# A hybrid diffusion block on one Trainium2 core: the low part of most weight tiles comes from an accumulating DMA instead of a VectorE subtraction

## The chip, the core and the metric

The kernel runs on one core of a Trainium2 chip. The metric is the time of one execution on the device, in microseconds (us). The engines are named as the profile names them: PE is TensorE (PEld its weight loads), DVE is VectorE, ACT is ScalarE, POOL is GpSimd, SP is SyncE, which here only issues DMAs. L12 is line 12 of the kernel's file; before and after have their own line numbers.

## What is computed

One layer of a diffusion backbone over 512 latent tokens of width 1024, with 256 context tokens in front of a state-space scan. All weights are float32, and the result is compared with a float32 reference. Cut to what matters:

```python
z, xbc, dt_raw, cv_in, pool_in, gate_logits = split(h @ w_in)         # latent and context
y_ssd  = rms_norm(ssd_scan(silu(conv5(xbc)), dt) * silu(z)) @ ssd_w_out
y_conv = silu(layer_norm(depthwise_conv31(a * sigmoid(b)))) @ cv_w_out  # a, b = cv_in
y_pool = pool_mixer(pool_in)
g = sigmoid(gate_logits)
x = x + mod[2] * ((g0 * y_ssd + g1 * y_conv + g2 * y_pool) @ w_out)
x = x + mod[5] * ((silu(h2 @ w_gate) * (h2 @ w_up)) @ w_down)
return rms_norm(x, final_g)
```

The change touches how the tiles of `w_in`, `cv_w_out`, `ssd_w_out`, `w_out` and `w_down` are made ready for the matmuls.

## The kernel before

Activations lie with channels on the 128 partitions and tokens along the free dimension, 512 wide. Every product is made of two-part numbers: a float32 value is split into a rounded float32r part `hi` and the rest `lo`, and a product is `hi*hi + hi*lo + lo*hi`, three matmuls (`mm3`, L136 to L138). A weight tile has 128 output channels and 1024 inputs (768 for `wcv` and for each third piece of `wdn`), so a whole tile takes 8 times 3, that is 24, matmuls of 128x512.

`load_unit` (L117) makes such a tile: an SP DMA brings 512 KB from HBM into `raw` (tag "wr"), ACT rounds it to `hi` (tag "whi"), DVE subtracts, `lo = raw - hi` (tag "wlo"). Each tag has three buffers, so the parts of a tile can be written only when the matmuls of the tile three before it are done. In the program's text the stages are:

- start (to about 48 us): the modulation, the first norm, three tiles of `win` split by hand (`first_split`), which the change leaves alone;
- 50 to 325 us: tiles of `win` for convolution, pooling and `xbc` (L755), with DVE at work on the 31-tap convolution (`conv31`, L410), pooling and the 5-tap convolution (L702);
- 325 to 500 us: tiles of `win` for `z` and the gates (`spill_tile`), spilled to HBM, between them the scan (`ssd_gen`): per chunk a product `cb` on PE (L820), `cbd` on DVE (L826), `xd` on POOL (L830);
- 500 to 625 us: `wcv`, `wso` and `wout` tiles; beside them the spilled gates and branch sums come back (L975, L976), rows of `wada` are read for the second modulation (`ada`, L902), and `x`, `yd` are read;
- 625 to 835 us: the gate and up projections, which the change leaves alone (`ffn_unit`, `fast_pair`);
- 835 us to the end: the down projection, 24 pieces of `wdn`, then the last norm and the output.

The order of the work on each engine comes from a scheduler with priorities (`later` pushes work back; `tc.high_priority()` puts the rounding and subtraction of a tile early). Each engine then runs its own instructions in that order. POOL has 68 instructions: pads set to zero (L398, L462, L657, L760) and the eight `xd` products.

Of the kernel before, what the change touches and what calls it, by code (L numbers as in the profile page):

```python
# [10 lines left out]
AF = mybir.ActivationFunctionType  # L11
ALU = mybir.AluOpType  # L12
P = 128
# [14 lines left out]
I_CV, I_PL, I_XBC, I_Z, I_G1, I_G0 = 0, 12, 26, 38, 46, 54  # L28
# [25 lines left out]
def hybrid_block(ctx, tc, x, cx, cck, cc, wad, wada, vec, prm, cst, inv, onehot, win, wdt, wcv, wpl, wso, wout, wgu, wdn, out):  # L54
    nc = tc.nc
# [9 lines left out]
    V, S, PE = (Ordered(e) for e in (nc.vector, nc.scalar, nc.tensor))  # L65
# [7 lines left out]
    def nm(s):  # L73
        uid[0] += 1
        return f"{s}_{uid[0]}"

    def pt(pool, shape, tag, bufs, dt=F32):
        return pool.tile(shape, dt, tag=tag, name=nm(tag), bufs=bufs)

    def mmp():  # L80
        return pt(psum, [P, T], "mm", 3)
# [4 lines left out]
    def tmp():  # L86
        return pt(per, [P, T], "tmp", 4)
# [24 lines left out]
    def load_raw(src, n):  # L112
        raw = pt(per, [P, 1024], "wr", 3)
        nc.sync.dma_start(raw[:, :n], src)
        return raw

    def load_unit(src, n=1024, urgent=True):  # L117
        raw = load_raw(src, n)
        hi = pt(per, [P, 1024], "whi", 3, F32R)
        lo = pt(per, [P, 1024], "wlo", 3, F32R)  # L120
        with tc.high_priority():
            S.copy(hi[:, :n], raw[:, :n])  # L122
            if urgent:
                V.tensor_tensor(lo[:, :n], raw[:, :n], hi[:, :n], ALU.subtract)  # L124
        if not urgent:
            V.tensor_tensor(lo[:, :n], raw[:, :n], hi[:, :n], ALU.subtract)
        return hi, lo

    def split(dst_hi, dst_lo, src):
        S.copy(dst_hi, src)  # L130
        V.tensor_tensor(dst_lo, src, dst_hi, ALU.subtract)  # L131

    def mm3(o, w, col, rhs, first, last):
        hi, lo = w
        rh, rl = rhs
        PE.matmul(o, hi[:, col : col + P], rh, start=first, stop=False)  # L136
        PE.matmul(o, hi[:, col : col + P], rl, start=False, stop=False)  # L137
        PE.matmul(o, lo[:, col : col + P], rh, start=False, stop=last)  # L138
# [20 lines left out]
    def slot_a(dt=F32):  # L159
        return pt(f1, [P, 2, T], "A", 3, dt)  # L160
# [10 lines left out]
    def slot_c(dt=F32):  # L171
        return pt(f1, [P, 1024], "C5", 4, dt)
# [167 lines left out]
    V, S, PE = nc.vector, nc.scalar, nc.tensor  # L340
# [10 lines left out]
    def drain(gen):  # L351
        for _ in gen:
            pass

    @contextmanager
    def later(n):
        keep = tc.cur_priority
        tc.cur_priority = keep + n
        yield
        tc.cur_priority = keep  # L360

    def win_tile(i, bank=mmp):
        if pre:
            return pre.pop(0)
        w = load_unit(win[i])
        o = bank()
        for k in range(KT):
            mm3(o, w, k * P, hh[k], k == 0, k == KT - 1)
        return o
# [47 lines left out]
    def conv_steps(n, ins=None):  # L417
        with ExitStack() as st:
            st.enter_context(later(100000))
            if ins is not None:  # L420
                st.enter_context(tc.issue_after(ins.ins))
            while n and convs:
                if next(convs[0], 0) == 0:
                    convs.popleft()
                else:
                    n -= 1
# [325 lines left out]

    tails = []
    for q, i in enumerate((8, 9, 10, 11, 0, 1, 2, 3, 4, 5, 6, 7)):
        w = load_unit(win[I_XBC + q])  # L755
        o = mmp()
        for k in range(KT):
            mm3(o, w, k * P, hh[k], k == 0, k == KT - 1)
        pad = slot_c()
        nc.gpsimd.memset(pad[:, 0:2], 0.0)  # L760
        nc.gpsimd.memset(pad[:, 514:518], 0.0)
        S.copy(pad[:, 2:514], o)
        if i < 10:
            oc = mmp()
            for k in range(KT):
                mm3(oc[:, :TC], w, k * P, hc[k], k == 0, k == KT - 1)
            nc.gpsimd.memset(pad[:, 774:776], 0.0)
            S.copy(pad[:, 518:774], oc[:, :TC])
        conv_steps(CONV_STEPS_XBC[q], mark[-1])
        while len(tails) > TAILS_KEPT_XBC[q]:  # L770
            drain(tails.pop(0))
        tails.append(xbc_tail(i, pad))
        next(tails[-1], None)
# [121 lines left out]
    def ada(n=1):  # L895
        for _ in range(n):
            if not adas:
                return
            chunk, t = adas.popleft()
            raw = load_raw(wada[(chunk - 2) * 8 + t], 1024)  # L900
            i = chunk * 8 + t
            V.tensor_tensor_reduce(  # L902
                raw, raw, silb[0], 1.0, vc("b_ada", i), ALU.mult, ALU.add, mod_l[:, i : i + 1]
            )
# [22 lines left out]
    with later(100000):  # L927
        cvy = []
        for j in range(6):
# [3 lines left out]
            hi, lo = p[:, 0:T], p[:, T : 2 * T]  # L933
            split(hi, lo, f)
            cvy.append((hi, lo))
    with later(9000):
        for m in range(8):
            w = load_unit(wcv[m], 768)
            oc = mmp()
            for k in range(6):  # L940
                mm3(oc, w, k * P, cvy[k], k == 0, k == 5)
            sp = tmp()
            S.copy(sp, oc)
            nc.sync.dma_start(mrg[:, m, 1, :], sp)
            ada(1)
# [6 lines left out]
    for t in range(KT):  # L952
# [5 lines left out]
        hi, lo = pt(per, [P, T], "hh", 8, F32R), pt(per, [P, T], "hl", 8, F32R)  # L958
# [8 lines left out]
        mg.append((slot_w(F32R), slot_w(F32R)))  # L967

    for m in range(8):
        w = load_unit(wso[m])  # L970
        o = mmp()
        for k in range(KT):
            mm3(o, w, k * P, y_hl[k], k == 0, k == KT - 1)
        ga, mo = slot_a(), slot_c().rearrange("p (a b) -> p a b", b=T)
        nc.sync.dma_start(ga, gat[:, m])  # L975
        nc.sync.dma_start(mo, mrg[:, m])  # L976
        S.activation(ga, ga, AF.Sigmoid)
        V.tensor_tensor(mo[:, 1, :], mo[:, 1, :], ga[:, 1, :], ALU.mult)
        V.tensor_tensor(mo[:, 0, :], mo[:, 0, :], mo[:, 1, :], ALU.add)
        V.tensor_tensor(ga[:, 0, :], o, ga[:, 0, :], ALU.mult)  # L980
        V.tensor_tensor(mo[:, 0, :], mo[:, 0, :], ga[:, 0, :], ALU.add)
        mr = mo[:, 0, :]
        split(mg[m][0], mg[m][1], mr)
# [6 lines left out]
    def project(o, ws, rhs, sl):  # L990
        n = sum(kn for _, kn in ws)
        q = 0
        for w, kn in ws:
            for k in range(kn):
                mm3(o[:, sl], w, k * P, tuple(a[:, sl] for a in rhs[q]), q == 0, q == n - 1)
                q += 1

    def residual(m, o, gate, base, sl, q, ms=None):
        V.scalar_tensor_tensor(x1[:, m, sl], o[:, sl], gate, base[:, sl], ALU.mult, ALU.add)
        if ms is None:  # L1000
            sq_acc(acc[:, sl], x1[:, m, sl], m == 0, sl.stop - sl.start, q)
        else:
            S.activation(q[:, sl], x1[:, m, sl], AF.Square)
            PE.matmul(ms, mean, q[:, sl], start=False, stop=True)

    def rms_head(sl):
        ms = psp()[:, : sl.stop - sl.start]
        PE.matmul(ms, mean, acc[:, sl], start=True, stop=False)
        return ms

    def rms_tail(ms, sl):
        rnorm(ms, sl.stop - sl.start, acc[:, sl])

    def wout_tile(m):
        if m % 2 == 0:
            xp.append(slot_a())
            nc.sync.dma_start(xp[-1], x[:, m : m + 2, :])
        return load_unit(wout[m]), mmp()

    xp, up = [], []  # L1020
    nh = 8 - WOUT_HALVED
# [16 lines left out]
    for m in range(nh):  # L1038
        if m < 2:
            o = pair[m][1]  # L1040
        else:
            w, o = wout_tile(m)
# [185 lines left out]
    for q in range(NFF // 2):  # L1228
# [3 lines left out]
        for e in range(2):  # L1232
            if tags:
                hi, lo = (a[:, e, :] for a in pair)
            else:
                hi, lo = (pt(per, [P, T], "hh", 8, F32R) for _ in range(2))
# [5 lines left out]
    for m in range(8):  # L1242
        ada(1)
        o = mmp()
        ws = [(load_unit(wdn[m, :, k0 * P : (k0 + kn) * P], kn * P), kn) for k0, kn in ((0, 8), (8, 8), (16, 6))]
        for sl in halves if m == 7 else whole:
            ms = rms_head(sl) if m == 7 else None
            project(o, ws, hid, sl)
            residual(m, o, mod_l[:, 40 + m : 41 + m], x1[:, m, :], sl, pt(per, [P, T], "hl", 8), ms)
            S.activation(x1[:, m, sl], x1[:, m, sl], AF.Copy, scale=fin_n[:, m : m + 1])  # L1250
            if m < 7:
                continue
            rms_tail(ms, sl)
            n = T // 2
            for q in range(4):
                ot = pt(f2, [P, 2, n], "hid", NFF)
                V.tensor_tensor(
                    ot, x1[:, 2 * q : 2 * q + 2, sl], acc[:, sl].unsqueeze(1).to_broadcast([P, 2, n]), ALU.mult
                )
                nc.sync.dma_start(out[:, 2 * q : 2 * q + 2, sl], ot)  # L1260
# [124 lines left out]
```

## Time and profile before

| | before |
|---|---|
| median of 3 runs | 984.8 us (983.79 to 985.79) |
| the profiled execution | 984.63 us |
| its span in the trace | 982.9 us |
| PE busy | 961.0 us (98%) |
| DVE busy | 781.8 us (80%) |
| ACT busy | 465.6 us (47%) |
| POOL busy | 20.7 us (2%) |
| DMA queue of SP | 143.23 MB, 43.8% of 16 engines' span |

The span runs from the first to the last instruction of the trace; 1.7 us of the execution lie around it. A busy PE in this table is not a PE at its peak: a 128x512 matmul is shown as 0.39 us long, but the next one starts 0.23 us later. "Share" of DMA is the mean busy share of the core's 16 DMA engines.

### The profile page before, as it was taken

Reading aid. Unit: us, or ns where it says so; the run is one execution under the profiler, and the core shown is the slowest. Engines: PE = TensorE matmul, PEld = TensorE weight load, DVE = VectorE, ACT = ScalarE, POOL = GpSimd, SP = SyncE. Lnnn points to the kernel's source line nnn. Section 1 sums busy time; section 2 is a strip of 40 time slices with the busy share of each in tenths; the row PEclk is TensorE's granted clock in tenths of the full one; section 3 lists DMA queues with packets and bytes.
Section 4 is the critical chain, followed back from the end, with each engine's and each line's share of the span. In section 5 each row is a group of like instructions: output and inputs, shape, how many; then the busy total and the mean of one; then the engine's idle time right before and its main releaser. Section 6 shows DMA issues by size and latency. Waiting matters only on the chain.

```text
span 982.9 us, 14243 instructions
## 1 busy us (share of the span) xinstructions
PE 961.0 (98%) x5468; PEld 807.9 (82%) x5468; DVE 781.8 (80%) x1196; ACT 465.6 (47%) x710; POOL 20.7 (2%) x68
## 2 busy tenths in 40 slices
PE   6999999999999999999999999999999999999996
PEld 4678888888887777766688788989999999888885
DVE  5589999977889999999987864999888888743333
ACT  5683643335445243245664544655555556432331
POOL 0100000000000000100100000000000000000000
PEclk9999999999999999999999999999999999999998
DMA  9653335322123356654769963233233333443422
GB/s 363 268 184 103 115 115 161 107 86 65 65 59 102 108 177 221 201 165 141 217 227 305 340 207 126 86 108 120 96 109 107 108 108 107 128 148 107 139 81 86
DMA packets 59157, 144.15 MB, mean 147 GB/s; under 512 B 11728, under 2 KB 22608, under 8 KB 57936
## 3 DMA queue, kind: packets, MB, share of 16 engines
q1 hardware_dynamic: 59088, 143.23, 43.8%
q8 instruction: 43, 0.70, 0.3%
q14 instruction: 26, 0.21, 0.1%
HBM read 126.44 MB, written 16.78 MB: 146 GB/s over the span
## 4 chain that ended last, share of the span: by engine, by line
PE 88%; DVE 5%; DMA 3%; ACT 1%; issue 1%; SPq 0%; DVEq 0%; ACTq 0%
PE mm L137 19%; PE mm L136 19%; PE mm L138 19%; PE mm L1162 10%; PE ps L1162 8%; PE mm L63 1%; DMA wr<-in_wso_dram 1%; PE ps L1079 1%; PE ps L796 1%; DMA wr<-in_wada_dram 1%; PE y L866 1%; PE ps L855 1%; PE ps L63 1%; PE ps L748 1%; DVE A L410 1%
## 5 line engine op out<-in xcount | busy, mean ns | idle before, releaser
L138 PE MATMUL mm<-hh,wlo 128*128 128x512 f32 (+1 forms) x612 | 242.5, 396 | 0.5 <-DVE wlo L124 0.5
L136 PE MATMUL mm<-hh,whi 128*128 128x512 f32 (+1 forms) x612 | 242.3, 396 | 0.3 <-ACT whi L122 0.3
L137 PE MATMUL mm<-hl,whi 128*128 128x512 f32 x576 | 230.2, 400 | 0.0
L122 ACT CAST whi<-wr 128x1024 fp32r<-128x1024 f32 (+1 forms) x115 | 117.0, 1021 | 237.6 <-PE mm L137 184.4
L124 DVE TENSOR_TENSOR wlo<-wr,whi 128x1024 fp32r<-128x1024 f32 (+1 forms) x112 | 132.0, 1181 | 54.5 <-ACT whi L122 54.0
L138 PEld LDWEIGHTS mm<-hh,wlo 128*128 128x128 f32 x612 | 115.2, 188 | 28.8 <-issue 4.3
L136 PEld LDWEIGHTS mm<-hh,whi 128*128 128x128 f32 x612 | 115.2, 188 | 27.3 <-issue 3.0
L137 PEld LDWEIGHTS mm<-hl,whi 128*128 128x128 f32 x576 | 108.4, 188 | 26.0 <-issue 4.3
L410 DVE SCALAR_TENSOR_TENSOR A<-U,vec_t,A 128x512 f32<-128x512 f32 x180 | 128.0, 752 | 0.0
L1162 PE MATMUL mm<-T,shi 128*128 128x256 f32 x288 | 53.5, 283 | 0.0
L130 ACT CAST shi<-S 128x1024 fp32r<-128x1024 f32 x36 | 37.8, 1050 | 31.8 <-DVE S L1150 26.1
L702 DVE SCALAR_TENSOR_TENSOR C<-C,vec_t,C 128x772 f32<-128x772 f32 (+1 forms) x48 | 46.9, 977 | 4.8 <-ACT C L700 2.2
L131 DVE TENSOR_TENSOR slo<-S,shi 128x1024 fp32r<-128x1024 f32 x36 | 44.1, 1225 | 5.9 <-ACT shi L130 5.9
L1162 PEld LDWEIGHTS mm<-T,shi 128*128 128x128 f32 x288 | 44.9, 191 | 0.0
L130 ACT CAST whi<-wr 128x1024 fp32r<-128x1024 f32 (+1 forms) x36 | 30.1, 836 | 25.9 <-PE ps L1162 21.2
L1162 PE MATMUL mm<-T,slo 128*128 128x256 f32 x144 | 40.9, 284 | 0.0
L131 DVE TENSOR_TENSOR wlo<-wr,whi 128x1024 fp32r<-128x1024 f32 (+1 forms) x36 | 34.5, 958 | 7.1 <-ACT whi L130 5.5
L136 PE MATMUL mm<-H,whi 128*128 128x256 f32 (+1 forms) x124 | 37.4, 302 | 0.0
L137 PE MATMUL mm<-H,whi 128*128 128x256 f32 (+1 forms) x124 | 37.3, 300 | 0.0
L138 PE MATMUL mm<-H,wlo 128*128 128x256 f32 (+1 forms) x124 | 37.2, 300 | 0.0
L902 DVE CUSTOM_DVE_ANT_0 wr<-wr,C,vec_t 128x1024 f32<-128x1024 f32 x24 | 30.7, 1279 | 1.0 <-DMA wr<-in_wada_dram 0.9
L902 DVE CUSTOM_DVE_ANT_0 wr<-wr,sil_f,vec_t 128x1024 f32<-128x1024 f32 x8 | 10.3, 1283 | 23.6 <-DMA wr<-in_wada_dram 23.6
(396 smaller groups left out, 2070.7 us busy)
## 6 DMA issues: line engine op xcount, KB each, us to landing
wr<-in_win_dram SPq DMA_DIRECT2D x62, 512.0 KB
wr<-in_wgu_dram SPq DMA_DIRECT2D x44, 512.0 KB
wr<-in_wada_dram SPq DMA_DIRECT2D x32, 512.0 KB
wr<-in_wdn_dram SPq DMA_DIRECT2D x16, 512.0 KB
X<-in_wad_dram SPq DMA_DIRECT2D x4, 1024.0 KB
H<-in_wad_dram SPq DMA_DIRECT2D x4, 1024.0 KB
mrg<-tmp SPq DMA_DIRECT2D x16, 256.0 KB
gat<-tmp SPq DMA_DIRECT2D x16, 256.0 KB
```

The lines of the kernel that those rows point to most:

```text
L63: return lambda *a, **k: tc.keep_in_program_order(op(*a, **k))
L122: S.copy(hi[:, :n], raw[:, :n])
L124: V.tensor_tensor(lo[:, :n], raw[:, :n], hi[:, :n], ALU.subtract)
L130: S.copy(dst_hi, src)
L131: V.tensor_tensor(dst_lo, src, dst_hi, ALU.subtract)
L136: PE.matmul(o, hi[:, col : col + P], rh, start=first, stop=False)
L137: PE.matmul(o, hi[:, col : col + P], rl, start=False, stop=False)
L138: PE.matmul(o, lo[:, col : col + P], rh, start=False, stop=last)
L410: V.scalar_tensor_tensor(accs[e], pads[e](k), vc("dw_w", (2 * j + e) * 31 + k), accs[e], ALU.mult, ALU.add)
L702: tap = V.scalar_tensor_tensor(a[:, 0:n], pad[:, k : n + k], vc("conv_w", i * 5 + k), a[:, 0:n], ALU.mult, ALU.add)
L902: V.tensor_tensor_reduce(raw, raw, silb[0], 1.0, vc("b_ada", i), ALU.mult, ALU.add, mod_l[:, i : i + 1])
L1162: PE.matmul(o[:, left], x[:, cs], rhs[k][y], start=first and k + n == 0, stop=k == 3 and n == 2, skip_group_check=True,)
```

## The change

`load_unit` gets a flag `rmw`, set at six of its callers: the tiles of `win` that are not split by hand (59), of `wcv` (8), `wso` (8), `wout` (8) and the pieces of `wdn` (24), 107 in all. With the flag ACT writes `hi` as before and then a second pass, `lo = -raw`, rounded in the same way by the float32r output; then a DMA issued by POOL reads the same weight tile from HBM once more and adds it to `lo`. The five tiles of the plain gate and up projections that are not first (`urgent`) keep the DVE subtraction.

```diff
-    def load_unit(src, n=1024, urgent=True):
+    def load_unit(src, n=1024, urgent=True, rmw=False):
         raw = load_raw(src, n)
         hi = pt(per, [P, 1024], "whi", 3, F32R)
         lo = pt(per, [P, 1024], "wlo", 3, F32R)
+        if rmw:
+            with tc.high_priority():
+                S.copy(hi[:, :n], raw[:, :n])
+                S.activation(lo[:, :n], raw[:, :n], AF.Copy, scale=-1.0)
+            nc.gpsimd.dma_start(lo[:, :n], src, accum_op=ALU.add)
+            return hi, lo
...
-        w = load_unit(win[i])
+        w = load_unit(win[i], rmw=True)
...
-        w = load_unit(win[I_XBC + q])
+        w = load_unit(win[I_XBC + q], rmw=True)
...
-            w = load_unit(wcv[m], 768)
+            w = load_unit(wcv[m], 768, rmw=True)
...
-        w = load_unit(wso[m])
+        w = load_unit(wso[m], rmw=True)
...
-        return load_unit(wout[m]), mmp()
+        return load_unit(wout[m], rmw=True), mmp()
...
-        ws = [(load_unit(wdn[m, :, k0 * P : (k0 + kn) * P], kn * P), kn) for k0, kn in ((0, 8), (8, 8), (16, 6))]
+        ws = [(load_unit(wdn[m, :, k0 * P : (k0 + kn) * P], kn * P, rmw=True), kn) for k0, kn in ((0, 8), (8, 8), (16, 6))]
```

The scheduler places the new instructions, and it shifts others around them. ACT at the `wso` tiles, before: `wr_...` are the raw tiles, `A_...` the gates, `C_...` the merged rows that become `H_...`.

```order
L977 ACTIVATE A_4743<-A_4743 128x1024
L130 CAST H_4618<-C_829_4660 128x512
L122 CAST whi_4756<-wr_4754 128x1024
L977 ACTIVATE A_4785<-A_4785 128x1024
L130 CAST H_4618<-C_835_4702 128x512
L122 CAST whi_4798<-wr_4796 128x1024
```

The same place after:

```order
L983 ACTIVATE A_4813<-A_4813 128x1024
L136 CAST H_4685<-C_829_4728 128x512
L123 CAST whi_4869<-wr_4867 128x1024
L124 ACTIVATE wlo_4870<-wr_4867 128x1024
L136 CAST H_4685<-C_835_4771 128x512
L983 ACTIVATE A_4856<-A_4856 128x1024
L983 ACTIVATE A_4899<-A_4899 128x1024
```

Behind each rounding of a tile now stands the second pass, which writes `wlo`; the other ACT work keeps its place but for one gate pass.

POOL between the pads of the scan's set-up (`M_...`, L657 before and L663 after) and those of the pooling (`X_...`), before:

```order
L657 MEMSET M_900 128x512
L657 MEMSET M_904 128x512
L657 MEMSET M_932 128x512
L657 MEMSET M_936 128x512
L462 MEMSET X_459 128x256
L463 MEMSET X_459 128x256
```

And after, from the last two accumulating DMAs ahead of the fourth pad:

```order
L125 DMA wlo_1108<-in_win_dram 128x1024
L125 DMA wlo_1152<-in_win_dram 128x1024
L663 MEMSET M_941 128x512
L125 DMA wlo_1198<-in_win_dram 128x1024
L125 DMA wlo_1253<-in_win_dram 128x1024
L468 MEMSET X_459 128x256
L125 DMA wlo_1287<-in_win_dram 128x1024
L469 MEMSET X_459 128x256
```

Accumulating DMAs that PE waits for now stand in one row with pads that wait for PE and DVE.

PE at the first tile that `load_unit` makes (`mm_472` before, `mm_473` after; `ps_567`, `ps_568` is the small product for `dt`), before:

```order
L63 MATMUL mm_209<-hh_95,wlo_345 128x512
L273 MATMUL ps_567<-W_106,C_61_269 32x512
L136 MATMUL mm_472<-hh_81,whi_468 128x512
L137 MATMUL mm_472<-hl_82,whi_468 128x512
L138 MATMUL mm_472<-hh_81,wlo_469 128x512
```

And after:

```order
L279 MATMUL ps_568<-W_116,C_61_269 32x512
L279 MATMUL ps_568<-W_118,C_61_269 32x512
L279 MATMUL ps_568<-W_120,C_61_269 32x512
L142 MATMUL mm_473<-hh_81,whi_468 128x512
L143 MATMUL mm_473<-hl_82,whi_468 128x512
L144 MATMUL mm_473<-hh_81,wlo_469 128x512
```

All eight products for `dt` now stand ahead of the tile; of each tile the third matmul is the first that reads `wlo`.

## Rows read from the trace of the kernel before

**Rows 1.** Page, busy time of each engine: us, share of span, instructions.

```profile
PE 961.0 (98%) x5468; PEld 807.9 (82%) x5468; DVE 781.8 (80%) x1196; ACT 465.6 (47%) x710; POOL 20.7 (2%) x68
```

**Rows 2.** Waits of PE: total us, times, longest.

```profile
PE ps L63 <- DMA X<-in_wad_dram: 8.2, 2, 7.2
PE mm L1162 <- DVE wlo L131: 1.3, 1, 1.3
...
PE ps L796 <- DVE W L794: 0.5, 2, 0.4
PE mm L138 <- DVE wlo L124: 0.5, 1, 0.5
```

**Rows 3.** Busy time by stage: from:to, length, engines, PEclk, DMA share, GB/s.

```profile
50.00:325.00 275.00, 274.61 (x1409) 228.24 (x1408) 248.49 (x370) 130.02 (x199) 5.42 (x46) 1.00 0.34 104
325.00:500.00 175.00, 174.46 (x801) 123.95 (x800) 165.25 (x271) 77.13 (x117) 11.91 (x8) 1.00 0.55 177
500.00:575.00 75.00, 74.21 (x326) 60.44 (x325) 60.29 (x88) 40.44 (x53) 0.00 (x0) 1.00 0.90 313
575.00:625.00 50.00, 49.91 (x293) 44.23 (x292) 26.96 (x47) 25.06 (x43) 0.00 (x0) 1.00 0.31 105
835.00:960.00 125.00, 124.95 (x579) 104.03 (x578) 56.99 (x74) 41.40 (x54) 0.00 (x0) 1.00 0.38 120
```

**Rows 4.** Costliest groups: the subtraction, the rounding, the scaled pass.

```profile
L122 ACT CAST whi<-wr 128x1024 fp32r<-128x1024 f32 (+1 forms) x115 | 117.0, 1021 | 237.6 <-PE mm L137 184.4
L124 DVE TENSOR_TENSOR wlo<-wr,whi 128x1024 fp32r<-128x1024 f32 (+1 forms) x112 | 132.0, 1181 | 54.5 <-ACT whi L122 54.0
L977 ACT ACTIVATE A<-A 128x1024 f32<-128x1024 f32 x8 | 8.5, 1061 | 10.0 <-DMA A<-gat 9.8
```

**Rows 5.** The subtractions (L124) of each stage.

```profile
50.00:325.00 275.00, 46.84 (x39) 1.00 0.34 104
325.00:500.00 175.00, 25.94 (x22) 1.00 0.55 177
500.00:575.00 75.00, 17.09 (x16) 1.00 0.90 313
835.00:960.00 125.00, 28.37 (x25) 1.00 0.38 120
```

**Rows 6.** SP's DMA queue, 500 to 575 us: packets, MB, share.

```profile
q1 hardware_dynamic: 7785, 23.38, 89.9%
```

**Rows 7.** Chain of waits, 500 to 545 us: start, us, what.

```profile
517.20 5.29 DMA wr<-in_wada_dram
522.51 1.28 DVE wr L902
...
524.54 8.18 DMA wr<-in_wso_dram
...
535.21 6.09 DMA wr<-in_wso_dram
541.38 1.06 ACT whi L122
542.46 1.24 DVE wlo L124
```

**Rows 8.** A load in the down projection: its issue on SP, its reader.

```profile
873.10 0.33 SPq L114 DMA_DIRECT2D wr<-in_wada_dram  x1
...
876.61 1.28 DVE L902 CUSTOM_DVE_ANT_0 wr<-wr,sil_f,vec_t 128x1024 f32<-128x1024 f32 x1 [3.55 <-DMA wr<-in_wada_dram]
```

**Rows 9.** ACT in order of time: roundings that wait for a free buffer.

```profile
45.52 1.05 ACT L122 CAST whi<-wr 128x1024 fp32r<-128x1024 f32 x1 [0.58 <-PE mm L63]
...
93.00 1.05 ACT L122 CAST whi<-wr 128x1024 fp32r<-128x1024 f32 x1 [2.57 <-issue]
98.49 1.05 ACT L122 CAST whi<-wr 128x1024 fp32r<-128x1024 f32 x1 [4.45 <-PE mm L137]
...
103.94 1.04 ACT L122 CAST whi<-wr 128x1024 fp32r<-128x1024 f32 x1 [3.90 <-PE mm L137]
...
861.18 1.05 ACT L122 CAST whi<-wr 128x1024 fp32r<-128x1024 f32 x1 [4.39 <-PE mm L137]
865.26 0.84 ACT L122 CAST whi<-wr 128x768 fp32r<-128x768 f32 x1 [3.03 <-PE mm L137]
```

**Rows 10.** PE and POOL in order of time, around the waits of POOL.

```profile
48.39 1.05 PE L273 MATMUL ps<-W,C 128*32 128x512 f32 x2
...
106.93 0.52 POOL L657 MEMSET M<- 128x512 f32 x1 [64.80 <-PE ps L668]
...
361.77 1.87 POOL L830 TENSOR_TENSOR W<-X,cbd 128x512 f32<-128x512 f32 x1 [31.57 <-DVE cbd L826]
```

## The prediction

> **What bounds the kernel now.** I read the busy times of the engines first. PE is busy for 98% of the span, DVE for 80%, ACT for 47%, POOL for 2% [rows 1]. The waits of PE come next, because a busy PE can still be held up between two matmuls. They are 8.2 us at the start for `wad`, which the change leaves alone, 1.3 us on L131 in the gate and up part, which it also leaves alone, and 0.5 us each on `W` and on the subtractions of L124 [rows 2]. So PE sets the end, its clock is granted in full in every stage (PEclk 1.00 [rows 3]), and nothing that DVE does now costs PE more than about 2 us in all. The stages then show where there is room on the other engines and on DMA. The DMA share is 0.34, 0.55, 0.31 and 0.38 in four of them, but 0.90 from 500 to 575 us [rows 3]. There the transfers are all but full while PE still does not wait. A change that adds DMA traffic must be read from that stage.
>
> **What goes away.** 107 of the 112 subtractions of L124 go, at 1.18 us each [rows 4]: 126 us of DVE. By the waits of PE they can return at most 0.5 us for L124, 0.5 for `W` and perhaps a little of L131: I take 2 us as the most and put all of it in the sum. The other 124 us lie beside matmuls.
>
> **What ACT gets.** 107 passes over a raw tile. Their form is not in the trace; the nearest rows are the rounding of the same tile, 1.02 us, and a scaled pass of the same size, 1.06 us [rows 4], so 109 to 113 us, and ACT goes from 466 to about 577 us of 983. Between roundings ACT is idle: in steady work it rounds a tile at 93.00, 98.49 and 103.94 us, waiting each time for the buffer that PE gives back [rows 9]. A pass of 1.05 us in each of these 5.5 us is hidden; without that cover it would be 1.05 us per tile, which is inside the latency term below.
>
> **What DMA gets.** 107 more reads of a weight tile, 512 KB each (384 KB for `wcv` and the third pieces), about 54 MB on top of 143. Its price is not in the trace, so I bound it from the stage that is nearly full. There the SP queue moved 23.38 MB in 89.9% of 75 us [rows 6], that is 67.4 us at a full share, 347 GB/s, or 1.51 us per 512 KB. The stage has 16 of the subtractions [rows 5], 5 of them of 384 KB: 14.75 whole tiles. If an accumulating transfer costs as much as a plain load, 14.75 x 1.51 = 22 us are added, and 67.4 + 22.3 = 89.7 us must fit into 75: 14.7 us more at a share of 1, 25 us at the share of 0.90. If the engines must also read the old `lo` as they read the tile, each costs two loads: 67.4 + 44.6 = 112 us, which is 37 us more at a share of 1 and 49 at 0.90. Below zero I exclude: the transfers come on top and none is removed. I take the second price, because an addition has two operands and a load has one, and 40 us, nearer to a full share, because 0.90 is reached there while PE does not wait, so it need not be the ceiling. Both ends stay for the range.
>
> The other stages hold the traffic even at that price. From 50 to 325 us 0.34 x 275 = 94 us plus 39 tiles x 3.02 = 118 make 212 of 275. From 325 to 500 us 0.55 x 175 = 96 plus 22 x 3.02 = 66 make 162 of 175, and from 835 to 960 us 0.38 x 125 = 48 plus at most 25 x 3.02 = 76 make 124 of 125 [rows 3, 5]. These two are full then, and not over.
>
> A rule of the Trainium skill speaks to the price. Its page "Collectives: The Full Stack", section "The bandwidth ceiling: the fold count and why AG ≠ RS ≠ AR", says that an addition on the way of a transfer needs two source reads on one ring, and gives 32.35 GB/s for it against 62.28 for a copy, a ratio of 1.93. By that figure the stage would hold 67.4 + 1.93 x 22.3 = 110 us, 35 over; by the only rows that there are, those of plain loads, it would be 14.7 over. The page measured this between cores, and no run here shows it yet.
>
> **What the tile's path gets.** Before, `lo` is ready 1.05 + 1.18 us after the raw tile may be rounded. After, it is 1.05 + 1.05 + about 0.5 for two handoffs + R, where R is the time from POOL's issue to the landed sum. R is not in the trace. The nearest rows are plain loads: issued at 873.10 with the reader at 876.61, so 3.5 us where DMA has room [rows 8], and 5.3, 8.2 and 6.1 us in the chain of waits at the crowded stage [rows 7]. So `lo` takes 6.1 to 10.8 us. It may take long, since three buffers let the rounding of a tile start when the tile three before it ends, and the tile is first read by PE two tiles later. One matmul takes 5.47 / 24 = 0.228 us (the roundings 5.47 us apart [rows 9], 24 matmuls a tile), and `lo` is read by the third, so 2 x 5.47 + 0.46 = 11.4 us are there for a tile of `win`. With that and R up to 8.2 nothing waits: 0. For the down projection the three pieces of an output tile take 66 matmuls, 15.05 us, and `lo` is held for 5.0 us from its first reader on. At R = 8.2 a buffer's round is 10.8 + 5.0 = 15.8 us, 0.8 over, and 8 rounds cost 6 us; at R = 3.5 they cost 0. In that stage ACT does wait for PE's buffers, as in the rows at 861.18 and 865.26 [rows 9]. I take 6, since the stage becomes as crowded as the one of [rows 7].
>
> At the first tile there is no lead. Its rounding runs at 45.52 [rows 9], so `lo` is there at 45.52 + 6.1 to 10.8: 51.6 to 56.3 us. PE comes to the tile after the products for `dt`, which start at 48.39 [rows 10] and of which all eight now stand ahead (8 x 0.23 = 1.9 us), and after two matmuls more it asks for `lo`, at about 50.8. The stall is 1 to 5.5 us; I take 3.
>
> **What stands in a row on POOL.** An accumulating DMA now waits behind pads and `xd`. The pad of `M` waited 64.80 us and ran at 106.93 behind a product of PE [rows 10]; the DMA of `wlo_1198` is next behind it. On PE at least 56 matmuls, 12.9 us, stand between that product and the first reader of `wlo_1198`, more than R, so 0. An `xd` as at 361.77 (it waited 31.57 us for `cbd` [rows 10]) also has some 53 matmuls, 12 us, between its `cb` product and the first reader of the tile behind it. That is cover for R up to about 8 us and not beyond; if it is gone, the rest of R counts once for each of eight, and I put that into the third rival.
>
> **The sum.** From the profiled execution, 984.63 us (0.2 below the median of 984.8; span 982.9 and 1.7 around it): 984.6 + 40 (crowded stage) + 3 (first tile) + 6 (down projection) - 2 (DVE) = 1032 us. The forecast is 1032: 37 or 49 for the stage, 0 to 6 for the pieces, 1 to 5.5 for the first tile give 1015 to 1048, its lower end set by a stage that hands some 10 us of its loads on to the part from 575 to 625 us (share 0.31 [rows 3]).
>
> **The rivals.** First, the accumulating DMA costs no more than a load: 984.6 + 15 to 25 + 3 + 0 - 2 = 1000 to 1012, at the middle 1006. For it: nothing in the trace shows a second read. Against it: an addition needs the old value, which lies in SBUF.
>
> Second, the DMAs don't overlap as loads do, so R is far above 8 us, and all tiles go at the pace of their three buffers, (2.6 + R + 5.0) / 3 per `win` tile. At R = 9 that is 5.5 us, nothing yet. At 10.5 it is 6.05, so 0.55 x 59 = 32 us, and the pieces lose (18.1 - 15.05) x 8 = 24: with the stage 984.6 + 40 + 3 + 32 + 24 - 2 = 1082. At 12 it is 61 + 36, 1123. So 1048 to 1125. For it: the crowded stage shows 8.2 us even for a plain load [rows 7], and all 107 leave by one queue of POOL. Against it: the other stages have DMA at half or less.
>
> Third, on the other side: not slower. The crowded stage is crowded by choice of order. Rows of `wada` for the second modulation are fetched in it, as at 517.20 [rows 7], and their readers on DVE (1.28 us each) get 17 us of room as 16 subtractions leave [rows 5]. With plain-load price the two stages from 500 to 625 us hold 67.4 + 0.31 x 50 + 34 = 117 us of transfers in 125 (34 for the 16 tiles there and up to 8 that follow, 22.75 x 1.51). If the loads that nobody awaits soon slip past 575 us, PE sees none of it, and the time is 984.6 - 2 to + 2, 983 to 987. It decides if the weights of `wso` and `wout` go ahead of those rows. Against it: SP issues in one fixed order, and the chain of waits in that stage runs over loads of `wada` and then of `wso`, so a late row holds up a late weight.
>
> That the change does not take the subtractions off DVE is not a rival: in the new order 5 of the 112 are left.
>
> **How the numbers follow.** A measurement of this kernel can tell about 0.2%, 2 us, from no change. Chances: the forecast 0.45 (1015 to 1048), the load's price 0.25 (1000 to 1015), no overlap 0.18 (1048 to 1125), not slower 0.12 (983 to 987, of it 0.03 below 982.8, since only the 2 us from DVE could bring it, and 0.09 within 0.2%). The range of 1000 to 1085 holds the first two whole and somewhat over half of the third, 0.80 in all; it leaves out the not slower side. Faster 0.03, same 0.09, slower 0.88.
>
> **What would show it.** In the changed profile the stage from about 500 us should be some 40 us longer with a DMA share near 0.9 or above, and PE's waits should name DMA for `wlo` or `raw` there. POOL's queue should show about 54 MB, and its packets' time against SP's tells one load's price from two. DVE should be near 656 us, ACT near 577. R is seen from the second pass on ACT to the first reader of `lo`. Should PE wait for `wlo` evenly in all stages, R is the cause and the second rival holds. Should the share from 500 us not rise, the traffic was not the bound. The forecast is wrong if PE's waits stay below 10 us in all, or if the additional time lies from 50 to 325 us, where I put 3.

## The result, and the profile after

The changed kernel takes 1078.2 us (1075.4 to 1080.1, 4 runs) against 984.8: 1.095 times the time of before, interval 1.092 to 1.097. That is 93 us more where 47 were forecast. The profiled execution has a span of 1075.9 us, 93.0 above the 982.9 of before.

The engines' busy times on the page of the changed kernel, beside [rows 1], then its DMA queues and two lines of its DMA issues (the last number is the median time from issue to landing in us):

```profile
PE 990.9 (92%) x5468; PEld 821.4 (76%) x5468; DVE 667.3 (62%) x1089; ACT 559.0 (52%) x815; POOL 113.2 (11%) x175
...
q1 hardware_dynamic: 59088, 143.23, 39.2%
q0 software_dynamic: 15408, 54.01, 28.2%
...
wlo<-in_win_dram POOLq DMA_DIRECT2D x59, 512.0 KB, 8.0
...
wlo<-in_wdn_dram POOLq DMA_DIRECT2D x16, 512.0 KB, 7.8
```

The work moved much as forecast: DVE has 667 us (656 were forecast), ACT 559 (577), POOL's queue carries 54.01 MB. The price of that queue can be read off. It held the DMA engines for 28.2% of 1075.9 us, 303 us, that is 2.95 us per 512 KB. SP's queue held them for 39.2%, 422 us, for 143.23 MB, 1.54 us per 512 KB. An added byte costs 1.9 times the engine time of a loaded one.

The waits of PE in the changed kernel, beside [rows 2] (total us, times, longest):

```profile
PE ps L885 <- DVE W L883: 12.6, 4, 4.0
PE mm L144 <- DMA wlo<-in_wso_dram: 10.6, 3, 5.5
PE mm L144 <- DMA wlo<-in_wcv_dram: 9.0, 4, 3.4
PE mm L144 <- DMA wlo<-in_wout_dram: 8.2, 4, 5.2
PE mm L144 <- DMA wlo<-in_win_dram: 7.6, 2, 4.8
...
PE ps L802 <- DVE W L800: 4.3, 3, 2.1
PE mm L144 <- DMA wlo<-in_wdn_dram: 3.0, 6, 0.7
PE mm L142 <- ACT tmp L458: 3.0, 1, 3.0
PE ps L199 <- DVE sum L160: 2.3, 1, 2.3
```

Three kinds stand in it. PE waits for `wlo` itself, mostly in the tiles of `wso`, `wcv` and `wout`, which was forecast. PE waits for DVE, which lost 114 us of work: that was not. And once it waits 3.0 us for ACT, of which more below. Waits are not all of it: with the same 5468 matmuls PE is busy for 990.9 us instead of 961.0, so about 30 of the 93 us show as slower matmuls and about 63 as idle time (the ends of matmuls are modelled, so the split is rough).

To see where the time went, the n-th of the three-part matmuls (`mm3`) in one trace is set against the n-th in the trace of before, and the growth of the delay is read between fixed points. Worked out in this way, in us, for all kernels of this study, each from one profiled execution (the stages are those of before: up to the start of the first `mm3`, then to about 176, 337, 480, 613 and 965 us):

| | first tile | to 176 | to 337 | scan, to 480 | crowded, to 613 | to the end | sum |
|---|---|---|---|---|---|---|---|
| changed kernel | 4.3 | 5.8 | 7.2 | 37.6 | 32.2 | 5.5 | 92.6 |
| tiny_sum | 4.0 | -1.9 | 0.3 | 11.6 | 5.2 | -0.3 | 18.8 |
| plain_load | 4.6 | 2.2 | 0.3 | 14.6 | 13.4 | 0.4 | 35.5 |
| half_sum | 4.1 | 4.3 | 0.3 | 20.6 | 15.2 | -0.3 | 44.1 |
| scan_off | 4.3 | 5.9 | 4.4 | 0.0 | 43.4 | 5.5 | 63.5 |
| scan_only | 1.2 | 0.0 | 0.0 | 34.7 | -6.7 | -0.1 | 29.0 |
| crowd_only | 0.6 | 0.0 | -0.1 | 0.0 | 44.0 | -0.3 | 44.2 |
| wdn_only | 0.2 | 0.0 | 0.0 | 0.7 | -0.1 | 5.1 | 5.9 |
| early_only | 3.9 | 5.9 | 4.1 | -0.1 | -0.2 | -0.1 | 13.5 |
| row_unread | 4.4 | 5.8 | 7.2 | 7.6 | 39.2 | 9.0 | 73.2 |
| raw_ring_4 | 5.0 | 8.8 | 0.3 | 33.4 | 35.3 | 1.9 | 84.7 |
| ring_4096 | 4.8 | 8.6 | 5.2 | 37.2 | 33.7 | 6.4 | 96.0 |
| pool_free | 3.7 | 7.4 | 0.1 | 34.9 | 37.8 | 6.3 | 90.2 |

A column holds everything that PE does between two fixed points, and the scheduler moved some of it. PE between the fixed points of the scan stage (from:to, length, busy time of PE, PEclk, DMA share, GB/s) before, in the changed kernel and in `row_unread`:

```profile
336.71:479.32 142.61, 142.07 (x646) 1.00 0.57 183
...
354.11:534.39 180.28, 158.89 (x679) 0.93 0.75 204
...
354.08:504.44 150.36, 148.44 (x697) 1.00 0.91 241
```

Small products of the scan that stood behind the point at 480 us now stand ahead of it: some 32 in the changed kernel, `plain_load` and `scan_only`, some 50 in `tiny_sum`, `half_sum`, `row_unread` and `raw_ring_4`. By their steps in the trace of before they take about 5 and 6 us. So much of the scan column is no loss, and the crowded column is too low by as much; the -6.7 of `scan_only` is mostly this. Below, a loss is called corrected when these products are counted where they stood before.

The changed kernel's stages (from:to, length, busy time of PE, PEld, DVE, ACT and POOL, PEclk, DMA share, GB/s), beside [rows 3]:

```profile
50.00:342.00 292.00, 279.01 (x1402) 230.62 (x1395) 207.78 (x335) 167.17 (x238) 38.83 (x84) 0.98 0.70 167
342.00:545.00 203.00, 181.61 (x784) 126.28 (x783) 139.22 (x245) 94.57 (x138) 29.35 (x30) 0.94 0.75 202
540.00:712.00 172.00, 144.13 (x658) 117.77 (x656) 68.80 (x118) 89.06 (x124) 20.03 (x23) 0.94 0.86 247
920.00:1060.00 140.00, 136.72 (x652) 112.41 (x651) 34.57 (x54) 66.08 (x86) 20.95 (x24) 1.00 0.82 192
```

Corrected, the scan stage lost about 33 us and the crowded stage about 37, and the scan stage lost them at a DMA share of only 0.75.

### The profile page after: what moved, and what is told of

The parts are those of the page before. It is cut to its first block, busy times and chain, and to the rows that moved or that the text cites. A ratio compares the mean times of both kernels' runs of the same rounds, so it can differ in the third digit from the quotient of the medians.

```text
span 1075.9 us, 14457 instructions
## 1 busy us (share of the span) xinstructions
PE 990.9 (92%) x5468; PEld 821.4 (76%) x5468; DVE 667.3 (62%) x1089; ACT 559.0 (52%) x815; POOL 113.2 (11%) x175
## 3 DMA queue, kind: packets, MB, share of 16 engines
q1 hardware_dynamic: 59088, 143.23, 39.2%
q0 software_dynamic: 15408, 54.01, 28.2%
## 4 chain that ended last, share of the span: by engine, by line
PE 50%; issue 19%; DMA 17%; DVE 8%; ACT 3%; POOL 2%; SPq 1%; DVEq 0%; POOLq 0%; ACTq 0%
PE mm L144 9%; PE mm L142 9%; PE mm L143 9%; PE mm L1168 7%; DMA wr<-in_wada_dram 6%; PE ps L1168 6%; POOL wlo L125 2%; DMA wlo<-in_wout_dram 2%; DMA wlo<-in_wso_dram 2%; DVE A L416 2%; PE mm L63 1%; DMA wr<-in_win_dram 1%; DVE wr L908 1%; PE ps L1085 1%; DMA wr<-in_wgu_dram 1%
## 5 line engine op out<-in xcount | busy, mean ns | idle before, releaser
L144 PE MATMUL mm<-hh,wlo 128*128 128x512 f32 (+1 forms) x612 | 248.2, 406 | 18.3 <-DMA wlo<-in_wso_dram 10.6
L142 PE MATMUL mm<-hh,whi 128*128 128x512 f32 (+1 forms) x612 | 249.0, 407 | 3.0 <-ACT tmp L458 3.0
L143 PE MATMUL mm<-hl,whi 128*128 128x512 f32 x576 | 234.3, 407 | 0.0
L123 ACT CAST whi<-wr 128x1024 fp32r<-128x1024 f32 (+1 forms) x107 | 108.6, 1017 | 198.8 <-PE mm L143 131.6
L144 PEld LDWEIGHTS mm<-hh,wlo 128*128 128x128 f32 x612 | 118.8, 194 | 50.5 <-DMA wlo<-in_wso_dram 11.9
L143 PEld LDWEIGHTS mm<-hl,whi 128*128 128x128 f32 x576 | 111.9, 194 | 26.8 <-issue 3.9
L124 ACT ACTIVATE wlo<-wr 128x1024 fp32r<-128x1024 f32 (+1 forms) x107 | 109.1, 1021 | 0.0
L125 POOL DMA_DIRECT2D wlo<-in_win_dram x59 | 51.6, 875 | 372.5 <-ACT wlo L124 260.5
L125 POOL DMA_DIRECT2D wlo<-in_wdn_dram x24 | 20.9, 873 | 338.1 <-ACT tmp L1207 235.5
L137 DVE TENSOR_TENSOR slo<-S,shi 128x1024 fp32r<-128x1024 f32 x36 | 44.1, 1224 | 5.9 <-ACT shi L136 5.7
L136 ACT CAST whi<-wr 128x1024 fp32r<-128x1024 f32 (+1 forms) x36 | 30.1, 835 | 25.8 <-PE ps L1168 21.2
L137 DVE TENSOR_TENSOR wlo<-wr,whi 128x1024 fp32r<-128x1024 f32 (+1 forms) x36 | 34.4, 957 | 7.2 <-ACT whi L136 5.8
```

Of the source, the lines that this page charges most:

```text
L124: S.activation(lo[:, :n], raw[:, :n], AF.Copy, scale=-1.0)
L125: nc.gpsimd.dma_start(lo[:, :n], src, accum_op=ALU.add)
```

## The experiments

Two theories stood against each other. By the first, the addition takes the DMA engines twice as long as a load, and everything that waits for transfers gets late (contention). By the second, the path to `lo` is simply long: second pass, POOL, a DMA's fixed time (latency).

### The path without the bytes, and the bytes without the addition

```diff
-            nc.gpsimd.dma_start(lo[:, :n], src, accum_op=ALU.add)
+            nc.gpsimd.dma_start(lo[:, :32], src[:, :32], accum_op=ALU.add)
```

> The accumulating DMA brings only the first 32 of the 1024 columns of a tile (16 KB instead of 512 KB); the rest of the sum is left out. The second pass on ACT, the issue on POOL and the wait of the third matmul stay. Contention theory (the loss is the time that the doubled transfers take from the DMA engines): nearly all of the 93 us are gone, 985 to 1000 us are left, and in the scan stage DVE no longer waits for rows of wada. Latency theory (the loss is the longer path to lo: second pass, POOL, a DMA's fixed time, whatever it moves): at least half of the loss stays, 1030 us or more.

Measured: 1005.2 us (1.020, 1.017 to 1.023), between what the two theories had said. The sign named for the scan stage did not come: DVE still waited 10.7 us for rows of `wada` there.

```diff
-            nc.gpsimd.dma_start(lo[:, :n], src, accum_op=ALU.add)
+            nc.gpsimd.dma_start(lo[:, :n], src)
```

> The same 512 KB are brought by the same POOL DMA at the same place, but they overwrite lo instead of being added; the addition is left out. The order of PE is the same as in the changed kernel. Contention theory: a 4096-byte packet takes about 0.16 us as in the SP queue instead of 0.33, the 54 MB cost half as much of the DMA engines, and the time falls to 1010 to 1040 us, with the crowded stage and the scan stage both better than half. Latency theory: issue to landing shrinks by little over 1 us, and the time stays above 1060 us.

Measured: 1019.5 us (1.035, 1.032 to 1.038), as the contention theory had said.

```diff
-            nc.gpsimd.dma_start(lo[:, :n], src, accum_op=ALU.add)
+            nc.gpsimd.dma_start(lo[:, : n // 2], src[:, : n // 2], accum_op=ALU.add)
```

> The accumulating DMA adds only the first half of a tile's columns (256 KB); the other half of the sum is left out. If the price of the addition is time of the DMA engines, half a tile costs them what a whole plain load costs (about 1.4 us per transfer), and the time comes out where the plain load's did, 1010 to 1030 us. If it is the addition as such that holds others up, whatever its size, it stays above 1050 us.

Measured: 1030.6 us (1.046, 1.043 to 1.049), just above the 1010 to 1030 expected. POOL's queue on the page of `tiny_sum` (packets, MB, share of 16 engines):

```profile
q0 software_dynamic: 15408, 1.76, 3.1%
```

The same line of `plain_load`, with its issues for `win` (the last number is the time to landing):

```profile
q0 software_dynamic: 15408, 54.01, 15.8%
...
wlo<-in_win_dram POOLq DMA_DIRECT2D x59, 512.0 KB, 5.0
```

And the same line of `half_sum`:

```profile
q0 software_dynamic: 15408, 27.01, 15.9%
```

With the path alone, 20 of the 93 us are left; the bytes at a plain load's price bring 14 more, and the addition 59 more. The same 54.01 MB took 15.8% of the plain kernel's span of 1018.8 us, 161 us, 1.56 us per 512 KB, against 2.95 with the addition: 1.89 times. The Trainium skill's page "Collectives: The Full Stack", section "The bandwidth ceiling: the fold count and why AG ≠ RS ≠ AR", gives 1.93 for an addition on the way between cores; here, from HBM into SBUF, the runs agree within 3%. Half the bytes with the addition hold the engines as long as all of them without, 163 against 161 us, and cost 11 us more: most of the loss goes by engine time, and a smaller part by something else, which I did not separate. So three quarters of the loss go with the bytes, and the path alone holds for 20 us. That those three quarters are full engines is not shown by these kernels alone, since the median landing time of a `win` tile moves with the bytes too: 4.1 us in `tiny_sum`, 5.0 in `plain_load`, 5.5 in `half_sum`, 8.0 in the changed kernel. The growth is not in proportion: engine time of 161 us costs 34, of 303 us 93.

### Each stage by itself

> Only the 24 tiles of wcv, wso and wout get the accumulating DMA, the other 83 keep the subtraction. If the crowded stage is bound by its own transfers, the loss is there whatever comes before: with all stages it was 32 us, with the scan stage undisturbed 43 us, so 1017 to 1030 us. If it is a delay that was piled up before, below 1005 us.

> Only the 24 pieces of wdn get the accumulating DMA. Between the first and the last piece the changed kernel lost 5.5 us; alone it should be the same: 989 to 992 us, by waits for wlo of up to 0.8 us at the short pieces. If the loss came from a state that the earlier stages leave behind, it stays within 2 us of 984.8.

> Only the 35 tiles of w_in before the scan get the accumulating DMA. With all, 17 us were lost up to 354 us: 4 at the first tile, 6 at about 65 us, 7 at 184 us. If these are made there and not given back, about 1002 us; if later stages have room to take some of it back, 990 to 998 us.

> Only the 24 tiles of z and the gates get the accumulating DMA. With all, 37 us were lost in the scan stage, with these off 29 us were won in all. If the stage loses alone what it loses in the whole, 1015 to 1025 us; if the late rows need the pressure of the stages around it, below 1005 us.

> The tiles of the z and gate columns of w_in (those of the scan stage, 24 of the 107) keep the VectorE subtraction, all others are as in the changed kernel. The delay of matmul against matmul grew by 37 us in that stage, so about 1041 us if it is made there, and DVE no longer waits 32 us for rows of wada in it. If the delay is only carried in from the stages before, or if the crowded stage takes over what is saved, it stays above 1060 us.

The edit is the flag at the callers, as in `scan_off`:

```diff
-        w = load_unit(win[i], rmw=True)
+        w = load_unit(win[i], rmw=i < I_Z)
```

Measured: `crowd_only` 1028.7 (1.044, 1.042 to 1.046), `wdn_only` 990.8 (1.0057, 1.0041 to 1.0074), `early_only` 999.1 (1.014, 1.011 to 1.017), `scan_only` 1012.4 (1.028, 1.024 to 1.032), `scan_off` 1049.6 us (1.066, 1.062 to 1.069). Two are as expected; `early_only`, `scan_only` and `scan_off` lie between the values of their two theories. Against the kernel before, run beside them, the four stages cost 43.8 + 5.9 + 13.8 + 27.1 = 90.6 us of the 93 by themselves. So each loss is made, in the main, where it shows. `scan_off` gained 29 us, and the crowded stage then lost 43 by the table instead of 32; about 5 of these 11 us are the moved products, which in `scan_off` stand where they stood before. Why the rest came back was not tested. Of `crowd_only`, the windows of its stage (columns as above):

```profile
500.00:545.00 45.00, 35.27 (x134) 27.16 (x133) 21.80 (x37) 22.37 (x35) 6.11 (x7) 0.89 0.92 261
545.00:590.00 45.00, 34.60 (x133) 27.49 (x132) 15.74 (x25) 21.94 (x24) 5.21 (x6) 0.85 0.98 304
590.00:635.00 45.00, 37.30 (x154) 29.41 (x153) 14.16 (x21) 22.88 (x28) 6.08 (x7) 0.94 0.93 261
```

The DMA engines are at 0.92 to 0.98 for 135 us, DVE is idle for over 60% of them, and PE waits for `wlo`. With half the engine time per tile, in `plain_load`, the same stage lost 13.4 us (corrected, about 18). This stage is bound by transfers.

### What the scan waits for

In the scan stage the engines for DMA are not full on the mean, yet PE stops. The chain of waits of the changed kernel there (start, us, what):

```profile
364.88 9.01 DMA wr<-in_wada_dram
...
375.33 9.70 DMA wr<-in_wada_dram
385.06 1.28 DVE wr L908
...
386.35 0.22 DVE W L883
...
386.70 0.71 PE ps L885 x2
```

And DVE in order of time around it, with what it waited for in brackets:

```profile
380.22 0.42 DVE L882 TENSOR_TENSOR W<-W 128x256 f32<-128x256 f32 x1
385.06 1.28 DVE L908 CUSTOM_DVE_ANT_0 wr<-wr,C,vec_t 128x1024 f32<-128x1024 f32 x1 [4.42 <-DMA wr<-in_wada_dram]
...
386.27 0.29 DVE L883 TENSOR_TENSOR W<-W 128x128 f32<-128x128 f32 x1
```

L882 and L883 are two steps of the scan's norm, 0.7 us of work. Between them in DVE's queue stands a row of `wada` for the second modulation, which nothing reads before the `wout` tiles. It landed 9.70 us after its issue; DVE stood still for 4.4 us, then L883 ran, and PE's L885 had waited for it. In the whole stage:

```profile
DVE wr L908 <- DMA wr<-in_wada_dram: 32.0, 13, 4.7
```

Before, DVE did not wait for these rows between 340 and 500 us at all. Such waits of DVE are not yet a loss of PE: what counts is whether a step like L883 stands behind the row. To test it, the rows are fetched but not read:

```diff
+            if chunk < 5:
+                return
             V.tensor_tensor_reduce(
```

> The changed kernel, but VectorE does not read the 24 rows of wada that are fetched from the scan stage on (their part of the second modulation is left out); the rows are still fetched, in the same raw buffers. If VectorE, standing in its queue at a row that lands late, holds up the scan's W and so PE, the 37 us of the scan stage fall to 10 us or less: 1045 to 1055 us. If PE is held by the weight tiles themselves (raw tile or lo late), the time stays above 1065 us.

Measured: 1042.1 us in one run and 1059.0 in the other, too far apart for an exact total, but both well below 1078. The trace is of the slower one. In it the scan stage lost 7.6 us instead of 37.6 (corrected, about 2 instead of 33) at a DMA share of 0.91, with PE's waits from 345 to 540 us being:

```profile
PE mm L145 <- DMA wlo<-in_wcv_dram: 6.5, 2, 6.2
PE ps L886 <- ACT whi L124: 1.2, 1, 1.2
PE ps L803 <- DVE W L801: 0.7, 2, 0.4
```

The rows in DVE's queue carry about 30 us of the scan stage's loss. The waits for W are all but gone, though the engines for DMA are fuller. The edit takes away more than the wait. Each row's 1.28 us on DVE goes too; that is hardly the cause, since before DVE did the same rows and 22 subtractions besides in this stage [rows 5], and PE did not wait. And a row that nobody reads gives its raw buffer back as soon as it has landed; this was not tested by itself, and the next run bears on it. Is it the three raw buffers that make the rows late?

```diff
-        raw = pt(per, [P, 1024], "wr", 3)
+        raw = pt(per, [P, 1024], "wr", 4)
```

> The changed kernel with four raw buffers (tag wr) instead of three; nothing is left out. If the scan stage loses because three buffers shared by weight tiles and rows of wada make their loads serial, each now 8 to 9 us, one buffer more lets the next load start earlier: 1040 to 1060 us. If the DMA engines are simply full there, or the wait is for lo, it stays within 10 us of 1078.

Measured: 1071.2 us (1.087, 1.084 to 1.091), 7 us less than the changed kernel and within the 10 us expected. The scan stage lost 33.4 (corrected, about 27), and DVE's waits for the rows from 345 to 540 us are nearly the same:

```profile
DVE wr L908 <- DMA wr<-in_wada_dram: 27.6, 13, 5.3
```

A fourth buffer helps little, so want of a place is at most a small part of why the rows are late.

### What stands behind what on POOL

POOL of the changed kernel around 180 us:

```profile
172.38 0.87 POOL L125 DMA_DIRECT2D wlo<-in_win_dram  x1 [6.16 <-ACT wlo L124]
180.98 0.31 POOL L469 MEMSET X<- 128x256 f32 x1 [7.72 <-DVE X L479]
183.50 0.31 POOL L468 MEMSET X<- 128x256 f32 x1 [2.21 <-DVE tmp L483]
184.13 0.86 POOL L125 DMA_DIRECT2D wlo<-in_win_dram  x1 [0.31 <-issue]
```

The second pass of that tile on ACT began at 175.97 and took 1.06 us; the DMA left at 184.13, because two pads of the pooling, which wait for DVE, stood ahead of it. Its sum landed 7.30 us later by the chain, and PE had waited 4.8 us.

```diff
-        nc.gpsimd.memset(pad[:, 0:4, :], 0.0)
+        V.memset(pad[:, 0:4, :], 0.0)
```

(The same at the other pads and at `xd`.)

> The changed kernel with the pads and xd on VectorE, so that POOL has nothing but the accumulating DMAs; nothing is left out. In the changed kernel a DMA at 184.13 us stood behind pads that waited for VectorE, and PE lost 7 us there: that loss is gone, the delay from 200 to 330 us falls from 17 to about 10 us, and the whole time to about 1071 us, or less if xd behind the DMAs costs in the scan. If the DMA was late there for another reason, 1076 to 1080 us.

Measured: 1073.6 us (1.090, 1.086 to 1.094). The loss between 176 and 337 us falls from 7.2 to 0.1, as expected of the place; the whole time falls by 4.6 us only, to between the two values expected. `xd` behind the DMAs cost little: the scan stage lost 34.9 with `xd` on DVE.

```diff
-    nc = bacc.Bacc("TRN2", target_bir_lowering=False, num_devices=1, dynamic_dma_scratch_size=1024)
+    nc = bacc.Bacc("TRN2", target_bir_lowering=False, num_devices=1, dynamic_dma_scratch_size=4096)
```

> The changed kernel with 4096 instead of 1024 bytes for the descriptors of POOL's DMAs; nothing is left out. If the room for descriptors makes one accumulating DMA wait for the one before, issue to landing falls below 6.5 us from 7.6 and the time by more than 10 us. If the price lies in the packets themselves (0.33 us for 4096 bytes), both stay: 1072 to 1084 us.

Measured: 1078.8 us (1.095, 1.092 to 1.098), and the page has 8.0 us from issue to landing as in the changed kernel. The room for descriptors is not it.

No kernel of these beats the one before: PE is 98% busy there, and each stage in which the addition stands loses.

## Why the prediction was right and wrong

The sign and the main mechanism held: transfers that cost two loads and a crowded stage bound by them. The forecast itself, 1032, was 46 us too low. That the time lies in the range is in part luck: 1078.2 is outside the forecast's own 1015 to 1048, and the range reached so far for the sake of the second rival, whose cause did not come. Of the terms, some came out near what was written, and three things were set to nothing and were not: the scan stage, the row on POOL, and a slower PE.

- **The price of the addition** was taken as two loads, and it is 1.9 (2.95 against 1.56 us per 512 KB). The first rival, one load, falls; and even at that price the time would have been 1019.5 and not 1006.
- **The crowded stage**, 40 us: 43.8 alone, 32.2 by the table (corrected, about 37) behind the late scan. Its time is bound by transfers, as worked out from its share.
- **The first tile**, 3 us: PE stood there for 5.7, above the upper end of 5.5. The 4.3 of the table is not this term: it ends at the first matmul, which does not read `lo`. That matmul waited for ACT's L458, which reads the result of an earlier tile and now stands behind second passes; `lo` was awaited at the third:

```profile
48.27 1.01 POOL L125 DMA_DIRECT2D wlo<-in_win_dram  x1 [5.75 <-ACT wlo L124]
...
49.72 2.00 ACT L124 ACTIVATE wlo<-wr 128x1024 fp32r<-128x1024 f32 x2
...
53.04 1.09 ACT L458 ACTIVATE tmp<-mm 128x512 f32<-128x512 f32 x2
...
53.69 0.50 PE L142 MATMUL mm<-hh,whi 128*128 128x512 f32 x1 [2.96 <-ACT tmp L458]
...
57.19 0.80 PE L144 MATMUL mm<-hh,wlo 128*128 128x512 f32 x1 [2.77 <-DMA wlo<-in_win_dram]
```

  The sum was there 8.9 us after its issue, above the 8.2 taken as the most for R. The second passes, called hidden, cost 3.0 us here, though without them the wait for `lo` would have been longer by about as much. The two handoffs, put at about 0.5 us without a row, took 0.34 and 0.05.
- **The down projection**, 6 us: 5.5 in the whole, 5.9 alone. The size came out, but not by the working: with R 7.8 the round of a buffer is 2.6 + 7.8 + 5.0 = 15.4 us against 15.05, and eight of them make 3 us. That is what PE waited for `wlo` of `wdn` (3.0); the rest was not separated.
- **The relief of DVE**, 2 us: not seen in any run.
- **The scan stage**, 0: it lost 37.6 by the table, about 33 corrected, and 27 by itself. The step that failed is the sentence that this stage has 162 us of transfers in 175 and so is full and not over. The sum was not too low (the share is 0.75). But PE does not wait there for the mean of the transfers; it waits for DVE, and DVE for single rows of `wada`, which it read 6 to 10 us after their issue where it waited for them up to 500 us. I had these rows in the third rival, as loads that could slip, and did not ask who is queued behind their readers on DVE.
- **The clock of PE**: the prediction reads it as granted in full before, and leaves it so in the sum. In the scan stage it was 0.93 on the mean, and PE was busy there for 16.8 us longer, of which about 5 are the moved products; over the whole kernel it was busy for 30 us longer. The last section shows one stop that cost more than its own length.
- **From 50 to 325 us**, 0 but for the first tile: the three columns up to 337 us hold 17.3. Some 8 are the first tile, its stops and the slow matmuls behind them, less 1 us of small products that now stand earlier. 7.2 are POOL's row of instructions: I priced the pad of `M` and `xd`, and passed over the pads of the pooling, which stand between DMAs in the order shown ahead of the prediction. The other 2.7 are the scan's mechanism once more: DVE stood 7.18 us at L600, a cast of a mask that its DMA brought late, with the convolution's L460 behind it, where before it had waited 1.02 us. L460's result goes through HBM, ACT's L159 waits for that DMA, and PE waited 2.3 us at L199 for what follows:

```profile
57.34 0.23 DVE L600 CAST msk<-W 128x128 int32<-128x128 f32 x1 [7.18 <-DMA W<-in_cst_dram]
57.48 0.68 DVE L460 TENSOR_TENSOR tmp<-mm,tmp 128x512 f32<-128x512 f32 x1
...
65.45 1.03 ACT L159 ACTIVATE tmp<-X 128x256 f32<-128x256 f32 x3 [5.98 <-DMA ud<-tmp]
...
67.53 0.67 PE L199 MATMUL ps<-sum,mean 128*128 128x256 f32 x2 [2.34 <-DVE sum L160]
```

- **The second rival**, R far above 8, named the time that came and not its cause: R was 8.0 at the median, and the tiles of `win` did not wait for their buffers' round, as the stretch from 200 to 337 us shows, where the delay did not grow.
- **The third rival** falls: nothing slipped without harm.
- **Sums.** Some ends do not follow from their terms. The first rival's terms give 1001 to 1011, not 1000 to 1012; the forecast's own give 1021 to 1043, or 1011 with the 10 us handed on, not 1015 to 1048; the second rival's are rounded by up to 2 us. None of this decides anything here.

What stays open: 20 us are lost with a sum of 32 columns (`tiny_sum`); of the 11.6 in its scan column about 6 are the moved products, so that, corrected, some 11 are lost in the crowded stage and 6 in the scan. The order on the engines differs there from before, and DVE waits for rows in that kernel too; which of the two costs them was not separated. Nor is the 11 us between `half_sum` and `plain_load`, nor how much of the whole loss is PE's clock.

## What to carry to other kernels

Price a transfer that adds at two loads (1.9 here), and ask of every load in the same stretch not whether the engines have room on the mean but which engine stands in its queue until that load has landed, and what of the critical path is queued behind it. An engine with less work is no help if it waits in order for something slower. Work that others wait for, on a queue with pads and set-up, inherits all their waits: read that queue's order row by row.

## What was not expected of the hardware

After a long stop PE did not go on at its old pace at once. Around the stop at 186 us, windows of the changed kernel (columns as above):

```profile
186.00:191.00 5.00, 0.62 (x3) 0.18 (x2) 4.99 (x8) 2.65 (x4) 0.86 (x1) 0.78 0.93 220
191.00:192.00 1.00, 0.53 (x1) 0.50 (x2) 0.97 (x4) 0.00 (x0) 0.00 (x0) 0.50 1.10 430
192.00:196.00 4.00, 4.00 (x11) 3.08 (x10) 4.00 (x9) 3.01 (x4) 0.97 (x4) 0.55 0.75 158
196.00:200.00 4.00, 4.00 (x19) 3.27 (x18) 1.55 (x3) 2.08 (x3) 0.10 (x3) 1.00 0.97 214
```

The granted clock fell to 0.50, the lower of its two levels (1.2 GHz), while PE had nothing to do, and 11 matmuls came in the next 4 us, 0.43 us apart by the chain instead of 0.23. So this stop of 4.8 us cost 7. Outside the scan the trace has 51 such slow steps more than that of before, about 10 of the 93 us.

An addition by DMA also took 3 us longer to land than the same transfer without it, 8.0 against 5.0 us at the median of the `win` tiles, and a load issued by SP needed 3.5 with room [rows 8].
